# A hybrid decoder layer on one core: when the down projection's inputs are loaded, and where the output projection's inputs lie

## The chip, the core and the metric

The kernel runs on one core of one Trainium2 chip. The metric is the time of one execution on the device in microseconds. Before the change three runs took 2108.03, 2109.98 and 2113.12 us, so the median is 2109.98 us.

The core has five engines with a queue of instructions each, worked off in program order: PE multiplies matrices, DVE does elementwise arithmetic, ACT copies, casts and applies functions, POOL does elementwise work and issues DMAs, SP issues DMAs. An instruction that waits holds up everything behind it on its own engine. In the profile's tables PEld is PE's loading of weights, and POOLq or SPq is the part of an engine that issues DMAs.

## The reference

A decoder layer of 512 tokens (and 16 meta tokens) of width 2048: one input projection, eight heads of stick-breaking attention beside a gated short convolution of 1024 channels, one output projection, and a feed-forward part (SwiGLU) of width 5632, all in float32.

```python
n = _rmsnorm(h, g_mix[l])
p = n @ w_in[l]
...
o = jnp.concatenate([_rmsnorm(o_attn, g_attn_out[l]),
                     _rmsnorm(o_conv, g_conv_out[l])], axis=-1)
h = h + o @ w_out[l]

n2 = _rmsnorm(h, g_ffn[l])
h = h + (jax.nn.silu(n2 @ w_gate[l]) * (n2 @ w_up[l])) @ w_down[l]
```

## The kernel before

**Three passes for one product.** Every float32 operand is split into a high part (a cast on ACT) and the low rest (a subtraction on DVE). A product is three matmuls: high x high, high x low, low x high (lines 670 to 672 and 684 to 686). Activations lie in memory transposed, tokens along the free dimension, with their high and low parts side by side.

**Output projection.** `wide_product` (line 664) works on 512 tokens at a time. The attention heads' outputs are `oa`, the convolution's `oc`, each one block of 8 x 2 x 512 numbers per partition, made by `o_slots` (line 288). Where in a partition such a block begins is set by small pad tiles ahead of it and by an offset inside the tile: `oa` begins 16 bytes into its tile, `oc` at the start of its own. The weights' split tiles `s` do not move. The two results are scaled and added to the residual, which gives `h`; from `h` come the inputs of the feed-forward part, split into seven combinations `acts[0]` to `acts[6]`.

**Seven products in place of eight.** The feed-forward products use a scheme in which a 2x2 block product needs seven block products. For every output pair (two output tiles) four quads of weights are loaded by SP: b11, b12, b21, b22 (`load_quad`, line 577), one buffer for each. DVE forms from them t1 = b11 + b12, then t2 from t1 and b22, t3 = b12 + b22, and adds b21 to t2 (`prepare_pair`, line 619; sums on lines 606 and 613). Each of the seven resulting weights is split on ACT (line 599) and DVE (line 600) into one of three buffers `s`, about two blocks ahead of PE. A quad's buffer is loaded for the next pair as soon as its last reader is done.

**A pair on PE.** `pair_product` (line 688) runs seven blocks into three accumulators: x with acts 0, z with 1, x with 2, z with 3, x with 4, y with 5, x with 6. Between them ACT copies partial results out and DVE combines them (lines 709, 713, 716); the sum on line 716 is `c1`, and it follows block y. For gate and up a block is 8 tiles of 128, 24 matmuls; there are 44 such pairs. The down projection runs in four chunks over the 5632 rows, `CHUNKS = (5, 6, 5, 6)` tiles a block, each chunk with eight pairs; a block is then 15 or 18 matmuls. Results of the first three chunks are added to `hd` in DRAM by accumulating DMAs from POOL (lines 956 and 957), those of the last go out.

**From gate/up to down.** After every pair `gate` (line 872) forms the product of silu and up and `store_acts` (line 862) splits it and stores it to DRAM tensors `fd[chunk][s]`, s being 0 to 6, by DMAs on POOL (two for an even tile, five for an odd one). The down projection reads them back into twelve ring places of SBUF by `load_acts(c, s)` (line 890), two DMAs on POOL each: part 0 holds the high, part 1 the low halves. A chunk uses seven places, the next chunk the following seven, in a circle.

- Place 0 lies free; chunk 0's slot 0 is loaded during gate/up (line 912).
- Places 1 to 5 lie over the gate/up inputs `f01` and `f25`. These are two tiles with two inputs each: acts 0 and 1, acts 2 and 5 (line 741). Their loads are written after the gate/up loop (lines 916 to 918), ahead of the last `gate`.
- Place 6 lies over acts 3 and 4, the others over acts 6 and the gate's work tiles.
- The next chunk's slots 0 to 4 are asked for in pairs 1 to 5 of a chunk (line 933), slots 5 and 6 after the last pair (line 942).

**Who orders.** The program is written as a stream; a scheduler at build time fixes each engine's order by readiness in its own model and by priority, and places the semaphores. A DMA written later can therefore stand earlier in POOL's queue than the text suggests. A tile that takes over memory waits for the last reader of the tiles that lay there.

Of the kernel before, what the change touches and what calls it, by code (L numbers as in the profile page):

```python
# [32 lines left out]
def hybrid_layer(ctx: ExitStack, tc: tile.TileContext, xT, w_in, w_out, w_gu, w_down, vecs, out):  # L33
# [247 lines left out]
    kns = [apool.tile([P, 640], F32, name=f"kn{i}") for i in range(1)]  # L281
    for t in kns:
        gp.memset(t[:, L:640], 0.0)
    oapool.tile([P, 8], F32, name="pad_oa")
    acc_c = oapool.tile([P, SEQ], F32, name="acc_c")
    acc_a = oapool.tile([P, SEQ], F32, name="acc_a")

    def o_slots(pool, name, at):

        t = pool.tile([P, 2 * HEADS * SEQ + 8], F32R, name=name)[:, at : at + 2 * HEADS * SEQ]  # L290
        return t.rearrange("p (h a t) -> p h a t", h=HEADS, a=2)

    oa_all = o_slots(oapool, "oa", 4)
    oa = []

    def halves(ps, n):
# [210 lines left out]
    for j in range(HEADS):  # L507
        pc = pp.tile([P, 2, 512], F32, tag="pp", name=f"pc{j}")
        product([(pc[:, 0, :CH], C0, C0 + CH), (pc[:, 1, :CH], C0 + CH, L)], n_hl)
        cu = t512(2 * CH, "e", 2)[:, : 2 * CH]  # L510
        ve.tensor_tensor(two(cu), halves(pc, CH), two(r2[:, C0:]), ALU.mult)
        pu = pp.tile([P, 2, 512], F32, tag="pp", name=f"pu{j}")
        product([(pu[:, 0, :CH], C0, C0 + CH), (pu[:, 1, :CH], C0 + CH, L)], n_hl)
        ve.tensor_tensor(two(cu), halves(pu, CH), two(cu), ALU.mult)
        y = t512(SEQ, "e2", 2)[:, :SEQ]
        sc.activation(y, cu[:, 2 : 2 + SEQ], AF.Copy, scale=cw[:, 3 * j : 3 * j + 1])
        for t in (1, 2):
            ve.scalar_tensor_tensor(
                y, cu[:, 2 + t : 2 + t + SEQ], cw[:, 3 * j + t : 3 * j + t + 1], y, ALU.mult, ALU.add
            )  # L520
        pb = pp.tile([P, 2, 512], F32, tag="pp", name=f"pb{j}")
        product([(pb[:, 0, :], META, L)], n_hl)
        gb = t512(SEQ, "v", 2)[:, :SEQ]
        ve.tensor_tensor(gb, pb[:, 0, :], r[:, META:], ALU.mult)
        gp.tensor_tensor(y, y, gb, ALU.mult)
        g = g_cnv[:, j : j + 1]
        if j == 0:
            assert not waiting
            after(10, scale_a)
            apool.release()  # L530
            ocpool = open_pool("ocpool")
            ocpool.tile([P, 32], F32, name="pad_oc")
            oc_all = o_slots(ocpool, "oc", 0)
        oh, ol = oc_all[:, j, 0], oc_all[:, j, 1]
        sc.activation(oh, y, AF.Copy, scale=g)
        ve.scalar_tensor_tensor(ol, y, g, oh.bitcast(F32), ALU.mult, ALU.subtract)
        square_sum(acc_c, y, j == 0)
        oc.append((oh, ol))
# [195 lines left out]
    def slot(pool, dt, n, tag, name):  # L734
        return slots(pool, dt, 1, n, name, tag=tag)[0]
# [2 lines left out]
        pool.tile([P, n // 4], F32, name=f"pad_{pool.name}")  # L738

    acts = {}  # L740
    for a, b in ((0, 1), (2, 5)):
        acts[a], acts[b] = slots(fpool, F32R, 2, 8, f"f{a}{b}")
    pad(fpool, 160)
    fx = {i: dram.tile([P, 2, 8, T2], F32R, name=f"fx{i}") for i in (3, 4, 6)}
    for _ in range(4):
# [2 lines left out]
    def wide_tmp(tag, dt=F32, bufs=1):  # L748
        n_tmp[0] += 1
        return hbuf.tile([P, SEQ], dt, tag=tag, bufs=bufs, name=f"w{n_tmp[0]}")  # L750

    def scale_c():
        w = (wide_tmp("t1", F32R), wide_tmp("t2", F32R), wide_tmp("h", bufs=2), wide_tmp("r"), wide_tmp("s"))
        token_scale(acc_c, acc_c, 1024, "c", w)

    after(3, scale_c)
# [1 line left out]
    for i, j in enumerate(OUT_TILES):  # L758
        hj = wide_tmp("h", bufs=2)
        gp.dma_start(hj, xT[j][:, META:])  # L760
        if i + 1 < KT:
            ps_out.append(pp.tile([P, 2, 512], F32, tag="pp", name=f"po{i + 1}"))
            wide_product(ps_out[i + 1][:, 0, :], oa)
            wide_product(ps_out[i + 1][:, 1, :], oc)
        ps = ps_out[i]
        t1, t2 = wide_tmp("t1"), wide_tmp("t2")
        half, k = divmod(j, 8)
        if half == 1:

            src = hbuf.tile([P, 8, T2], F32, tag="src", name=f"src{k}")  # L770

        def residual(eng):
            ve.tensor_tensor(t1, ps[:, 0, :], acc_a, ALU.mult)
            eng.tensor_tensor(hj, hj, t1, ALU.add)
            ve.tensor_tensor(t2, ps[:, 1, :], acc_c, ALU.mult)
            eng.tensor_tensor(hj, hj, t2, ALU.add)
            sc.activation(src[:, 2 * half : 2 * half + 2], two(hj), AF.Copy, scale=g_ffn[:, j : j + 1])

        def split_f(s, i):
            split(acts[s][:, 0, k], acts[s][:, 1, k], src[:, i])  # L780

        def mixed_blocks():
            split_f(0, 0)
            ve.tensor_tensor(src[:, 4], src[:, 3], src[:, 1], ALU.subtract)
            split_f(1, 4)
            ve.scalar_tensor_tensor(src[:, 5], src[:, 4], -1.0, src[:, 0], ALU.mult, ALU.subtract)
            split_f(2, 5)
            ve.scalar_tensor_tensor(src[:, 6], src[:, 5], -1.0, src[:, 2], ALU.mult, ALU.subtract)
            ve.tensor_tensor(src[:, 7], src[:, 0], src[:, 1], ALU.subtract)

        if i == KT - 1:
            with tc.high_priority(1 << 20):
                residual(ve)
                square_sum(acc_h, hj, False, wide_tmp("s"))
                mixed_blocks()
            ocpool.release()
            oapool.release()
            fp = open_pool("fp")
            rings_p = [open_pool("ring_0")]
            pad(rings_p[0], 32)  # L800
            rings, n_ring, ring = {}, [0], []

            groups = {0: (0, 1), 1: (1, 2), 3: (1, 1), 4: (1, 1), 5: (1, 1), 6: (2, 1), 7: (2, 5)}

            def ring_place():
                i = n_ring[0] % 12
                n_ring[0] += 1
                if i == len(ring):
                    p, m = groups[i]
                    ring.extend(slots(rings_p[p], F32R, m, 6, f"ring{i}", tag=f"ring{i}"))  # L810
                return ring[i]

            r0 = ring_place()
            fpool_last = open_pool("fpool_last")
            for s, n in ((3, 7), (4, 7), (6, 8)):
                acts[s] = slot(fpool_last, F32R, 8, f"f{s}", f"f{s}")
                for part in range(2):
                    gp.dma_start(acts[s][:, part, :n], fx[s][:, part, :n], max_dma_last_dim=4096)
            split_f(3, 6)
            split_f(4, 7)  # L820
        else:
            residual(gp if half else ve)
            if half:
                split_f(5, 2)
                st = hbuf.tile([P, 2, 2, T2], F32R, tag="st", name=f"st{j}")[:, :, 0]
                split(st[:, 0], st[:, 1], src[:, 3])
                gp.dma_start(fx[6][:, :, k], st)
            else:
                mixed_blocks()
                st = hbuf.tile([P, 2, 2, T2], F32R, tag="st", name=f"st{j}")  # L830
                split(st[:, 0], st[:, 1], src[:, 6:8])
                for n, s in enumerate((3, 4)):
                    gp.dma_start(fx[s][:, :, k], st[:, :, n])
        if i < KT - 1:
            square_sum(acc_h, hj, i == 0, wide_tmp("s"))
        hd = dram.tile([P, SEQ], F32, name=f"hd{j}")
        (gp if i < KT - 1 else nc.sync).dma_start(hd, hj)
        hs[j] = hd
# [23 lines left out]
    def store_acts(blks, n, slots, kp):  # L862

        t = apool.tile([P, 2, n, T2], F32R, tag=f"s{n}", name=f"s{kp}_{n}")
        split(t[:, 0], t[:, 1], blks)
        c, k = at[kp]
        for i, s in enumerate(slots):
            gp.dma_start(fd[c][s][:, :, k], t[:, :, i])  # L868

    even = [None]  # L870

# [15 lines left out]
            ve.scalar_tensor_tensor(odd[:, 4], odd[:, 3], -1.0, odd[:, 0], ALU.mult, ALU.subtract)  # L887
            store_acts(odd, 5, (5, 6, 1, 2, 3), f // 2)

    def load_acts(c, s):  # L890
        if c < len(CHUNKS):
            n = CHUNKS[c]
            rings[c, s] = (ring_place() if c or s else r0)[:, :, :n]

            for part in range(2):
                gp.dma_start(rings[c, s][:, part], fd[c][s][:, part], max_dma_last_dim=3072)
# [17 lines left out]


    rings_p.append(open_pool("ring_a", side="right"))
    for s in range(1, 6):
        load_acts(0, s)
    pad(rings_p[1], 160)
    gate(FT - 1, g1, u1, x)  # L920
    apool.release()
# [4 lines left out]
    for c in range(len(CHUNKS)):  # L926
# [3 lines left out]
            hh = slots(rings_p[1], F32, 1, 6, "hh", tag="ring4")[0]  # L930
        for j in range(KT // 2):

            if 1 <= j <= 5:
                load_acts(c + 1, j - 1)
            c1 = cpool.tile([P, 2, T2], F32, tag="c1", name=f"d1_{c}_{j}")
            c2 = cpool.tile([P, 2, T2], F32, tag="c2", name=f"d2_{c}_{j}")
            if end:
                h2 = [hh[:, :, 2 * (j % 3) + m] for m in range(2)]
                for m in (1, 0):
                    gp.dma_start(h2[m], two(hs[2 * j + m]))  # L940
            x = pair_product([rings[c, s] for s in range(7)], c1, c2)
            if j == KT // 2 - 1:
                for s in (5, 6):
                    load_acts(c + 1, s)
# [74 lines left out]
```

## Time and profile before

| what | us |
|---|---|
| median of three runs | 2109.98 |
| the profiled execution | 2107.92 |
| its span, first to last instruction | 2106.2 |
| output projection on PE (from the first `wide_product` matmul) | 638.4 to 804.3 |
| gate and up | 804.3 to 1656.8 |
| down, chunk 0 | 1656.8 to 1768.7 |
| down, chunk 1 | 1768.7 to 1884.4 |
| down, chunk 2 | 1884.4 to 1985.6 |
| down, chunk 3 | 1985.6 to 2102.1 |

Lines of the views are read so: line of the kernel, engine, operation, output<-inputs by the program's names without numbers (so `s`, `ring`, `b` stand for all tiles of that name), shapes, count; then busy time and mean duration of one in ns. In timelines the first two numbers are start and duration, and the bracket holds the engine's idle time before it and what ended that. Matmuls overlap one another, so the mean duration of one (275 ns) is longer than the distance from one to the next.

### The profile page before, as it was taken

The page shows a single profiled execution, that of the slowest core. Times are in us where ns is not written, and L with a number is a line of the kernel's source. Part 1 is how long each engine was busy: PE and PEld are TensorE (multiplying, and loading weights), DVE is VectorE, ACT ScalarE, POOL GpSimd, SP SyncE. Part 2 cuts the span into 40 slices and gives each one's busy share as a digit, 9 for nine tenths or more (in the row PEclk, how much of TensorE's full clock was granted, in tenths as well). Part 3 has the DMA queues.
Part 4 walks back from the last instruction along what each step waited for, and adds up shares of the span by engine and source line. Part 5 has one row for each costly group of instructions (what it writes and reads, how often), then busy time and mean ns, then how long its engine had stood idle before and what let it go on. Part 6 is the DMA issues. An engine that isn't in the chain of part 4 may idle for free.

```text
span 2106.2 us, 39382 instructions
## 1 busy us (share of the span) xinstructions
PE 2070.5 (98%) x16086; PEld 1987.5 (94%) x16086; DVE 1644.0 (78%) x2131; ACT 1019.5 (48%) x1576; POOL 458.9 (22%) x584
## 2 busy tenths in 40 slices
PE   8999999999999999999999999999999899999999
PEld 7999999999998888999999999999999899999999
DVE  8777767433337669999999998999989777877798
ACT  6666666322224344555555554555555444444443
POOL 4111111010003544122121221221111323122232
PEclk9999999999999999999999999999999999999999
DMA  5222222222235556566565565565554999788863
GB/s 173 81 72 80 74 78 81 81 97 94 91 110 172 177 181 221 166 184 179 172 190 166 154 193 165 172 178 160 170 153 146 304 280 278 202 232 246 241 190 121
DMA packets 146006, 342.48 MB, mean 163 GB/s; under 512 B 13393, under 2 KB 58961, under 8 KB 145825
## 3 DMA queue, kind: packets, MB, share of 16 engines
q1 hardware_dynamic: 67824, 214.33, 32.1%
q0 software_dynamic: 78000, 125.63, 21.9%
q8 instruction: 126, 2.06, 0.4%
q14 instruction: 56, 0.45, 0.1%
HBM read 268.60 MB, written 71.30 MB: 161 GB/s over the span
## 4 chain that ended last, share of the span: by engine, by line
PE 87%; DVE 5%; DMA 4%; issue 2%; ACT 1%; POOL 0%; SPq 0%; DVEq 0%; ACTq 0%
PE x L684 10%; PE x L686 9%; PE x L685 9%; PE z L684 5%; PE z L685 5%; PE z L686 5%; PE y L686 3%; PE y L685 3%; PE y L684 3%; PE po L671 3%; PE po L670 3%; PE po L672 3%; DMA b<-w_down 2%; DVE s L600 2%; PE pv L168 2%
## 5 line engine op out<-in xcount | busy, mean ns | idle before, releaser
L599 ACT CAST s<-t 128x1024 fp32r<-128x1024 f32 (+2 forms) x304 | 286.3, 942 | 395.3 <-PE z L686 127.6
L600 DVE TENSOR_TENSOR s<-t,s 128x1024 fp32r<-128x1024 f32 (+2 forms) x304 | 343.4, 1129 | 94.0 <-ACT s L599 92.5
L686 PE MATMUL x<-f,s 128*128 128x256 f32 x1408 | 387.3, 275 | 1.5 <-DVE s L600 1.5
L685 PE MATMUL x<-f,s 128*128 128x256 f32 x1408 | 387.4, 275 | 1.3 <-DVE f L183 1.3
L684 PE MATMUL x<-f,s 128*128 128x256 f32 x1408 | 387.3, 275 | 0.2 <-ACT f L182 0.2
L599 ACT CAST s<-b 128x1024 fp32r<-128x1024 f32 (+2 forms) x228 | 214.7, 942 | 221.7 <-PE x L686 202.1
L686 PEld LDWEIGHTS x<-f,s 128*128 128x128 f32 x1408 | 264.3, 188 | 1.7 <-DVE s L600 1.7
L685 PEld LDWEIGHTS x<-f,s 128*128 128x128 f32 x1408 | 264.3, 188 | 1.7 <-DVE f L183 1.5
L684 PEld LDWEIGHTS x<-f,s 128*128 128x128 f32 x1408 | 264.3, 188 | 0.5 <-ACT f L182 0.4
L600 DVE TENSOR_TENSOR s<-b,s 128x1024 fp32r<-128x1024 f32 (+2 forms) x228 | 248.1, 1088 | 3.1 <-ACT s L599 2.5
L137 DVE TENSOR_TENSOR wlo<-raw,whi 128x512 fp32r<-128x512 f32 (+1 forms) x198 | 142.3, 720 | 130.9 <-ACT whi L136 130.3
L868 POOL DMA_DIRECT2D fd<-s x154 | 108.8, 921 | 583.6 <-DVE s L183 582.1
L136 ACT CAST whi<-raw 128x512 fp32r<-128x512 f32 (+1 forms) x198 | 121.3, 614 | 185.3 <-PE pu L170 65.5
L684 PE MATMUL x<-ring,s 128*128 128x256 f32 x704 | 195.7, 278 | 8.6 <-DVE d L713 5.6
L684 PE MATMUL z<-f,s 128*128 128x256 f32 x704 | 195.8, 278 | 3.3 <-ACT p L705 3.1
L685 PE MATMUL x<-ring,s 128*128 128x256 f32 x704 | 194.8, 277 | 3.3 <-DMA ring<-fd 3.3
L686 PE MATMUL x<-ring,s 128*128 128x256 f32 x704 | 195.0, 277 | 0.4 <-DVE s L600 0.4
L686 PE MATMUL z<-f,s 128*128 128x256 f32 x704 | 193.9, 275 | 0.0
L685 PE MATMUL z<-f,s 128*128 128x256 f32 x704 | 193.9, 275 | 0.0
L606 DVE TENSOR_TENSOR t<-b,b 128x1024 f32<-128x1024 f32 (+2 forms) x152 | 166.4, 1094 | 27.8 <-DMA b<-w_down 23.2
L684 PEld LDWEIGHTS x<-ring,s 128*128 128x128 f32 x704 | 132.7, 189 | 10.7 <-issue 8.5
L684 PEld LDWEIGHTS z<-f,s 128*128 128x128 f32 x704 | 132.1, 188 | 6.5 <-ACT p L705 6.3
(326 smaller groups left out, 5599.0 us busy)
## 6 DMA issues: line engine op xcount, KB each, us to landing
b<-w_gu SPq DMA_DIRECT2D x176, 512.0 KB, 3.6
raw<-w_in SPq DMA_DIRECT2D x92, 512.0 KB, 3.3
fd<-s POOLq DMA_DIRECT2D x154, 256.0 KB, 5.3
b<-w_down SPq DMA_DIRECT2D x64, 384.0 KB, 3.9
ring<-fd POOLq DMA_DIRECT2D x28, 768.0 KB, 12.2
b<-w_down SPq DMA_DIRECT2D x64, 320.0 KB, 4.8
ring<-fd POOLq DMA_DIRECT2D x28, 640.0 KB, 11.3
wide<-w_out SPq DMA_DIRECT2D x30, 512.0 KB, 3.4
```

Of the source, the lines that this page charges most:

```text
L136: sc.copy(hi[:, :c], raw)
L137: ve.tensor_tensor(lo[:, :c], raw, hi[:, :c].bitcast(F32), ALU.subtract)
L599: sc.copy(hi, src)
L600: ve.tensor_tensor(lo, src, hi.bitcast(F32), ALU.subtract)
L606: ve.tensor_tensor(sums[name], a, b, ALU.add)
L670: pe.matmul(ps, hi[:, kk], ah, start=k == 0, stop=False)
L671: pe.matmul(ps, hi[:, kk], al, start=False, stop=False)
L672: pe.matmul(ps, lo[:, kk], ah, start=False, stop=k == 7)
L684: pe.matmul(ps, hi[:, kk], act[:, 0, k], start=start and k == 0, stop=False, skip_group_check=not start)
L685: pe.matmul(ps, hi[:, kk], act[:, 1, k], start=False, stop=False, skip_group_check=not start)
L686: pe.matmul(ps, lo[:, kk], act[:, 0, k], start=False, stop=k == n - 1, skip_group_check=not start)
L868: gp.dma_start(fd[c][s][:, :, k], t[:, :, i])
```

## The change

Four things, as one diff:

- `oa` and `oc` lose the offset inside their tiles, and the pad ahead of `oa` grows.
- The inputs acts 0, 1, 2 and 5 get a tile each; acts 3 and 4 now share one. A temporary of `scale_c` moves into the tile `st`, which makes room for this.
- The loads of chunk 0's slots 1 to 5 get the highest priority, and the stores of the last gate/up pair's two tiles go out on SP in place of POOL.
- The next chunk's slots 0 to 4 are asked for in pairs 2 to 6, and each first has two elements written by ACT, copied from the `c1` of the pair before, so that its DMAs wait for that sum.

```diff
-    oapool.tile([P, 8], F32, name="pad_oa")
+    oapool.tile([P, 48], F32, name="pad_oa")
...
-    def o_slots(pool, name, at):
+    def o_slots(pool, name):
-        t = pool.tile([P, 2 * HEADS * SEQ + 8], F32R, name=name)[:, at : at + 2 * HEADS * SEQ]
+        t = pool.tile([P, 2 * HEADS * SEQ], F32R, name=name)
         return t.rearrange("p (h a t) -> p h a t", h=HEADS, a=2)
-    oa_all = o_slots(oapool, "oa", 4)
+    oa_all = o_slots(oapool, "oa")
...
-            ocpool.tile([P, 32], F32, name="pad_oc")
-            oc_all = o_slots(ocpool, "oc", 0)
+            oc_all = o_slots(ocpool, "oc")
...
-    for a, b in ((0, 1), (2, 5)):
-        acts[a], acts[b] = slots(fpool, F32R, 2, 8, f"f{a}{b}")
+    for i in (0, 1, 2, 5):
+        acts[i] = slot(fpool, F32R, 8, f"f{i}", f"f{i}")
...
+        v = hbuf.tile([P, 2 * SEQ], F32, tag="st", name="scale_v")
-        w = (wide_tmp("t1", F32R), wide_tmp("t2", F32R), wide_tmp("h", bufs=2), wide_tmp("r"), wide_tmp("s"))
+        w = (wide_tmp("t1", F32R), wide_tmp("t2", F32R), wide_tmp("h", bufs=2), v[:, :SEQ], wide_tmp("s"))
...
             fpool_last = open_pool("fpool_last")
+            acts[3], acts[4] = slots(fpool_last, F32R, 2, 8, "f34")
+            acts[6] = slot(fpool_last, F32R, 8, "f6", "f6")
             for s, n in ((3, 7), (4, 7), (6, 8)):
-                acts[s] = slot(fpool_last, F32R, 8, f"f{s}", f"f{s}")
...
         for i, s in enumerate(slots):
-            gp.dma_start(fd[c][s][:, :, k], t[:, :, i])
+            if kp < FT // 2 - 1:
+                gp.dma_start(fd[c][s][:, :, k], t[:, :, i])
+            else:
+                nc.sync.dma_start(fd[c][s][:, :, k].bitcast(F32), t[:, :, i].bitcast(F32))
...
-    def load_acts(c, s):
+    def load_acts(c, s, behind=None):
         if c < len(CHUNKS):
             n = CHUNKS[c]
             rings[c, s] = (ring_place() if c or s else r0)[:, :, :n]
+            if behind is not None:
+                sc.copy(rings[c, s][:1, :, 0, 0], behind[:1, :2])
...
-    for s in range(1, 6):
-        load_acts(0, s)
+    with tc.high_priority(1 << 20):
+        for s in range(1, 6):
+            load_acts(0, s)
...
-            if 1 <= j <= 5:
-                load_acts(c + 1, j - 1)
+            if 2 <= j <= 6:
+                load_acts(c + 1, j - 2, c1_last)
...
             x = pair_product([rings[c, s] for s in range(7)], c1, c2)
+            c1_last = c1[:, 0]
```

## The prediction

> **What bounds the kernel now.** I read first the page: the matrix engine (PE) is busy for nearly the whole span, and the chain of waits that ended last runs through it.
>
> ```profile
> span 2106.2 us, 39382 instructions
> PE 2070.5 (98%) x16086; PEld 1987.5 (94%) x16086; DVE 1644.0 (78%) x2131; ACT 1019.5 (48%) x1576; POOL 458.9 (22%) x584
> PE 87%; DVE 5%; DMA 4%; issue 2%; ACT 1%; POOL 0%; SPq 0%; DVEq 0%; ACTq 0%
> ```
>
> So only PE's holes can be won, and the rate of its matmuls. Next I cut the down projection into windows: the first three chunks, then single pairs of chunk 0 (six of its eight), then four pairs of chunk 2. The 76 output pairs are numbered through: 0 to 43 are gate/up, 44 to 51 chunk 0, 52 to 59 chunk 1, 60 to 67 chunk 2. Columns: start and end, length, busy time of PE, PEld, DVE, ACT, POOL with counts, granted clock, DMA share, GB/s. Pair borders are where the first matmul of a pair starts.
>
> ```profile
> 1656.80:1768.70 111.90, 100.99 (x842) 98.31 (x841) 82.00 (x117) 51.35 (x90) 32.03 (x41) 0.98 0.99 286
> 1768.70:1884.40 115.70, 114.90 (x1010) 114.54 (x1009) 91.65 (x114) 55.34 (x88) 25.14 (x32) 1.00 0.85 231
> 1884.40:1985.60 101.20, 97.19 (x842) 96.05 (x842) 78.77 (x112) 49.69 (x88) 23.20 (x30) 1.00 0.87 246
> ...
> 1656.80:1672.90 16.10, 11.54 (x78) 10.55 (x76) 11.06 (x16) 7.22 (x12) 6.35 (x10) 0.89 1.26 393
> 1672.90:1690.90 18.00, 16.58 (x134) 15.79 (x135) 11.25 (x16) 6.81 (x12) 7.10 (x9) 1.00 1.14 341
> 1690.90:1704.90 14.00, 12.55 (x108) 12.19 (x107) 10.09 (x17) 6.18 (x11) 4.74 (x6) 1.00 1.11 326
> 1704.90:1718.20 13.30, 12.40 (x107) 12.03 (x106) 9.53 (x15) 6.18 (x11) 3.27 (x4) 1.00 1.12 358
> 1730.10:1742.00 11.90, 11.90 (x107) 11.90 (x107) 10.02 (x15) 6.19 (x11) 1.70 (x2) 1.00 0.67 155
> 1753.90:1768.70 14.80, 12.22 (x107) 12.05 (x107) 10.34 (x15) 6.40 (x11) 5.43 (x7) 1.00 1.04 306
> ...
> 1884.40:1897.60 13.20, 12.55 (x107) 12.19 (x107) 9.35 (x15) 6.18 (x11) 5.15 (x7) 1.00 1.14 364
> 1897.60:1912.00 14.40, 12.48 (x107) 12.11 (x106) 9.67 (x15) 6.17 (x11) 4.02 (x6) 1.00 1.13 365
> 1912.00:1925.00 13.00, 12.43 (x108) 12.18 (x107) 9.73 (x15) 6.18 (x11) 1.72 (x2) 1.00 0.89 248
> 1972.60:1985.60 13.00, 12.14 (x107) 11.97 (x106) 10.20 (x15) 6.40 (x11) 5.44 (x8) 1.00 1.04 324
> ```
>
> A quiet pair of five tiles takes 11.9 us with PE full (7 blocks of 15 matmuls, 113 ns each, 1.7 us a block). Eight would be 95.2, so chunk 0 loses 16.7 us and chunk 2 loses 6.0. Chunk 1, whose matmuls need 1008 x 113 ns = 114.3 us, loses 1.4. Every losing pair has DMA at 300 GB/s or more (or, at 1912.0, its tail); the quiet pair has 155. Two things are late there. In the first pair it is the activations themselves (PE, timeline):
>
> ```profile
> 1660.35 0.35 PE L684 MATMUL x<-ring,s 128*128 128x256 f32 x1
> 1662.81 0.58 PE L685 MATMUL x<-ring,s 128*128 128x256 f32 x1 [2.10 <-DMA ring<-fd]
> 1666.89 0.39 PE L685 MATMUL z<-ring,s 128*128 128x256 f32 x1 [0.58 <-DMA ring<-fd]
> 1670.22 0.38 PE L685 MATMUL x<-ring,s 128*128 128x256 f32 x1 [1.23 <-DMA ring<-fd]
> ```
>
> In the other pairs it is the weights: a quad from w_down lands 6.5 us after issue while ring loads flow, 3.5 us in quiet pairs, and DVE, which adds quads in program order, stands still. The DMA views are of 1640 to 1690 and of 1725 to 1755; then DVE's longest such wait.
>
> ```profile
> ring<-fd POOLq DMA_DIRECT2D x12, 640.0 KB, 11.3
> b<-w_down SPq DMA_DIRECT2D x11, 320.0 KB, 6.5
> ...
> b<-w_down SPq DMA_DIRECT2D x9, 320.0 KB, 3.5
> ...
> 1699.09 0.82 DVE L606 TENSOR_TENSOR t<-b,b 128x640 f32<-128x640 f32 x1 [2.93 <-DMA b<-w_down]
> ```
>
> That wait of 2.93 us stands in the pair that loses 2.1, so about 0.9 us of such a wait is absorbed by the weights split ahead.
>
> **Part 1, the first loads (slots 1 to 6 of chunk 0).** POOL's timeline of before:
>
> ```profile
> 1646.60 1.40 POOL L868 DMA_DIRECT2D fd<-s  x2 [12.85 <-DVE s L183]
> 1647.78 3.09 POOL L896 DMA_DIRECT2D ring<-fd  x4
> 1654.53 1.42 POOL L896 DMA_DIRECT2D ring<-fd  x2 [3.66 <-PE y L686]
> 1656.74 2.85 POOL L896 DMA_DIRECT2D ring<-fd  x4 [0.79 <-issue]
> 1665.97 3.54 POOL L868 DMA_DIRECT2D fd<-s  x5 [6.38 <-DVE s L183]
> 1672.88 0.94 POOL L956 DMA_DIRECT2D hd<-d  x1 [3.37 <-DVE d L713]
> 1673.46 1.83 POOL L896 DMA_DIRECT2D ring<-fd  x2
> ```
>
> Slots 1 and 2 stand behind two stores, slot 3 behind the end of block y (tile f25 is shared by acts 2 and 5), slot 6 behind five stores that wait for DVE's split and one accumulation. After: tiles of their own, stores on SP, and in the built program's POOL order the twelve DMAs stand together ahead of the first accumulation. Their waits follow the blocks of the last gate/up pair, 24 matmuls or 2.7 us each: y, the sixth, ends by 1654.5, so f1 is free at 1643.5 and f2 at 1646.2. Slots 1 and 2 gain 4 us, slot 3 gains 8, slots 4 and 5 stay bound to f5 (1654.5), slot 6 goes from 1673.5 to about 1658. In the quoted PE rows the last parts of slots 2, 3 and 4 arrive at 1662.8, 1666.9 and 1670.2: four parts in 7.4 us, 1.85 us each. The first part should land 4 to 8 us after its issue (a weight quad of half the size takes 3.5 to 6.5), so at that cadence the twelfth lands 20.4 us after a first landing at 1648 to 1652: 1668 to 1672. That stands against uses that without waits begin at 1658.5 (slot 1) and then every 1.7 us up to about 1668 (slot 6, which the built order puts behind 25 matmuls of the next pair and of y). What is left of waiting for ring is 0 to 3 us, and 5 if the cadence is a quarter slower. The two pairs now take 34.1 us, 10.3 over quiet. DVE's busy 11.06 + 11.25 = 22.3 us in them (the last gate's work is in it) leaves 1.5 us of 23.8, so they won't be quiet: weights are still contended and the casts hand over with gaps. I take 29.0 for both, **5.1 us won**; bounds 1 (weights and DVE hold them) and 8.
>
> The seven stores (1.40 + 3.54 us of POOL) cost POOL nothing any more. On SP the first two stand behind a weight load and ahead of b21 of pair 44, three ahead of b21 of pair 45, two ahead of b11 of pair 46. By the built order each waits for a DVE split that stands earlier on DVE than the read that frees the next quad's buffer, so SP loses only issue time; but 256 KB each now travel in the weights' queue. That may bring back up to 2 us, inside the bounds above.
>
> **Part 2, one load a pair.** It removes the bursts after pair 45 and in pairs 60 to 62. Pairs 46 and 47 lose 2.1 + 1.4, pairs 60 to 62 lose 1.3 + 2.5 + 1.1, and of chunk 1's 1.4 I count 0.4, for its first pairs: **8.8 us**. The bursts in pairs 51 (2.9) and 67 (1.1) stay, since slots 5 and 6 are still loaded together there.
>
> What it adds: ten pairs of five tiles (46 to 50, 62 to 66) and five of six tiles each get two parts. In the built order the first goes out after the c1 sum of the pair before, the second behind that pair's last accumulation, so both lie in the stretch where the next pair's b12 and b22 are loaded. No row of before shows this alone. Bounds: 0 (two parts of 1.85 us fit into a DMA share of 0.67 per 11.9 us) and pair 61's 2.5. I take **0.5 each**, nearer to nothing because the DMA is not full, but not nothing because DVE has 1.9 us free in such a pair: 10 x 0.5 = 5.0. For the six-tile pairs 0.15, as now: 0.8. Net of part 2: 8.8 - 5.8 = **3.0 us won**.
>
> The hold itself is 15 ACT copies of two elements. The nearest row is a 128x256 copy:
>
> ```profile
> 1742.92 0.36 ACT L955 COPY d<-x 128x256 f32<-128x256 f32 x1
> ```
>
> ACT is busy 6.19 of 11.9 us, and the c1 sum that a copy waits for is done by the time the cast ahead of it in the built order (the next t1) ends; so the cast of t2 behind it is held up by 0.36 us at most. Cost 0; 15 x 0.36 = 5.4 us if every copy fell on the path. On POOL only accumulations stand behind a held load.
>
> **Part 3, the output projection.** Rows: mean ns of a 512-column matmul.
>
> ```profile
> L671 PE MATMUL po<-oa,s 128*128 128x512 f32 x120 | 47.6, 397 | 0.0
> L670 PE MATMUL po<-oc,s 128*128 128x512 f32 x120 | 47.1, 392 | 0.0
> L670 PE MATMUL po<-oa,s 128*128 128x512 f32 x120 | 47.0, 392 | 0.0
> L672 PE MATMUL po<-oc,s 128*128 128x512 f32 x120 | 47.0, 391 | 0.0
> L671 PE MATMUL po<-oc,s 128*128 128x512 f32 x120 | 46.7, 389 | 0.0
> L672 PE MATMUL po<-oa,s 128*128 128x512 f32 x120 | 46.6, 388 | 0.0
> ```
>
> oa takes 397 + 392 + 388 = 1177 ns for its three, oc 1172. oc does not move (byte 54400 of a partition); oa goes from 21488 to 21632, now a whole number of 64 bytes and exactly 32 KB below oc. Placed alike it should run alike: 5 ns x 120 = **0.6 us won**. Bounds from the extreme rows: all at 388 wins 1.6, all at 397 loses 1.7. The gate/up tiles move as well, but keep their 16-byte offset, and the same matmul out of tiles at quite other places has nearly one price:
>
> ```profile
> L685 PE MATMUL x<-f,s 128*128 128x256 f32 x1408 | 387.4, 275 | 1.3 <-DVE f L183 1.3
> L685 PE MATMUL x<-ring,s 128*128 128x256 f32 x704 | 194.8, 277 | 3.3 <-DMA ring<-fd 3.3
> ```
>
> So that move costs 0. The combined tile f34 waits for oc's last matmul, where f3 alone waited for oa's; its first use is four blocks on, so it costs nothing. scale_v is read before anything that reuses st.
>
> **Sum.** 5.1 + 3.0 + 0.6 = 8.7 us off the profiled execution's 2107.92 (span 2106.2 and 1.7 around it): 2099.2. The median of the runs shown is 2.1 above that execution, so 2099.2 to 2101.3; I say **2100**. Less than 0.2% (4.2 us) from 2109.98 can't be told from no change.
>
> **Rivals.**
> (a) The spread loads vanish in idle DMA, and the start wins 8: 8 + 8.8 + 0.6 = 17.4, 2090.5. For it: share 0.67. Against it: DVE's small reserve.
> (b) The start is held by weights, not by ring: it wins 1, the rest stays, 4.6 in all: 2103 to 2105. For it: DVE's 22.3 of 23.8; against it: the three ring waits alone are 3.9 us.
> (c) Slower: any ring part in flight delays b12 and b22 as much as a burst does, at each of the ten five-tile boundaries. At pair 46's 2.1 this is 21 + 0.8 - 8.8 - 5.1 - 0.6 = 7.3 more: 2115 to 2117. It decides from 1.4 us a boundary (no gain) and is measurably slower from 1.8. For it: pair 47, with three parts, loses 1.4; against it: in bursts the queue held more than two parts.
> The Trainium skill's page "DMA: Bandwidth & Descriptors", section "Queues, rings and completion order", has each DMA engine turn from queue to queue packet by packet, so a weight load would share with the ring queue however deep that is. The landing of 6.5 against 3.5 agrees that sharing costs; that depth is irrelevant no run here shows yet. By that rule (c).
> (d) The loads don't come earlier, since a wait not seen holds them: 3.0 + 0.6, 2104 to 2106.
>
> **Chances.** Forecast (its own range 2095 to 2104) 0.48; (a) 0.18; (b) 0.11; (c) 0.16; (d) 0.07. Faster: the forecast and (a) whole, 0.09 of (b), 0.03 of (d), together 0.78. Slower: 0.12 of (c). No change: what is left, 0.10. The range 2089 to 2110 holds the forecast, (b), (d), some 0.6 of (a) and the mild end of (c), about 0.8.
>
> **What will show it.** POOL's ring issues beginning near 1643.5 with no store ahead; PE's ring waits in the first pair below 2 us in sum and no clock of 0.89; pairs 44 and 45 near 29 us; pairs 46 to 50 near 12.4 with b12 landing 4 to 6 us after issue; L671 on oa at 389. Pairs 46 to 50 at 13.3 or more would make it wrong.

## The result and the profile after

The changed kernel takes 2120.79 us in the median, the kernel before, run beside it, 2112.44 us: a ratio of 1.0041, 95% interval 1.003 to 1.0052. It is 8.4 us slower where 2100 was forecast. The profiled execution of the changed kernel took 2119.01 us; of its page:

```profile
PE 2069.0 (98%) x16086; PEld 1985.2 (94%) x16086; DVE 1642.5 (78%) x2131; ACT 1022.1 (48%) x1591; POOL 456.7 (22%) x577
PE 81%; DVE 8%; DMA 7%; issue 3%; ACT 2%; SPq 0%; DVEq 0%; POOL 0%; ACTq 0%
```

The busy times are those of before. What grew is the share of DVE and DMA in the chain of waits, from 9% to 15% of the span. The windows say where (same columns as in the prediction; here several pairs stand in one row):

```profile
1657.00:1687.50 30.50, 26.61 (x213) 24.91 (x213) 22.54 (x34) 14.09 (x25) 5.87 (x8) 1.00 1.01 315
1687.50:1757.80 70.30, 62.13 (x528) 60.59 (x527) 48.55 (x71) 31.70 (x59) 15.76 (x20) 1.00 0.87 244
...
1888.70:1912.50 23.80, 23.80 (x212) 23.80 (x211) 19.34 (x28) 12.48 (x23) 3.80 (x5) 1.00 0.68 156
1912.50:1982.90 70.40, 62.53 (x528) 60.71 (x527) 48.84 (x72) 31.68 (x59) 15.78 (x20) 1.00 0.89 243
```

The rows are pairs 44 and 45, 46 to 50, 60 and 61, and 62 to 66. Beside the lengths of the same pairs before:

| pairs | what is loaded meanwhile, after | before | after |
|---|---|---|---|
| 44, 45 | chunk 0's own slots | 34.1 | 30.5 |
| 46 to 50 | one held load a pair | 63.0 | 70.3 |
| 51 | slots 5 and 6 | 14.8 | 14.9 |
| 52 to 59 (six tiles) | one held load in five of them | 115.7 | 116.0 |
| 60, 61 | nothing (before: a burst) | 27.6 | 23.8 |
| 62 to 66 | one held load a pair | 60.6 | 70.4 |
| 67 | slots 5 and 6 | 13.0 | 13.9 |

The start of the down projection won 3.6 us, and the bursts in pairs 60 and 61 are gone, another 3.8. But every pair of five tiles that carries one held load takes 13.5 to 14.8 us in place of the quiet 11.9. The ten of them cost 7.3 + 9.8 = 17.1 us more than before. Over these pairs the DMA share is 0.87 to 0.89; while one of the loads is in flight it is 1.05 (1715 to 1724), just behind that 0.75 (1724 to 1728). What DVE waits for in pairs 46 to 50 (its sums on line 605, and one of these waits in the timeline):

```profile
L605 DVE TENSOR_TENSOR t<-b,b x11: 824/826/827, 1687.4 to 1757.7; 128x640 f32<-128x640 f32 x11
...
  DMA b<-w_down: 15.3, 8
...
1723.66 0.82 DVE L605 TENSOR_TENSOR t<-b,b 128x640 f32<-128x640 f32 x1 [3.09 <-DMA b<-w_down]
```

Eight waits for a weight quad, 15.3 us in all; PE loses 70.3 - 59.5 = 10.8 us, for part of each wait is absorbed by the weights split ahead.

The two profiled executions differ by 11.1 us, the medians by 8.4. Part of that is chance: the first two gate/up pairs took 45.3 us in the profiled execution of before and 49.0 in hold_only below, whose code is the same up to there. PE waits for `fx` loads in these two pairs in every profiled execution but that of before (0.2 to 3.6 us, in hold_only 1.8), so before's was a lucky one there.

### The profile page after: what moved, and what is told of

Its sections match the earlier page's. It is cut to its first block, busy times and chain, and to the rows that moved or that the text cites. A ratio compares the mean times of both kernels' runs of the same rounds, so it can differ in the third digit from the quotient of the medians.

```text
span 2117.3 us, 39408 instructions
## 1 busy us (share of the span) xinstructions
PE 2069.0 (98%) x16086; PEld 1985.2 (94%) x16086; DVE 1642.5 (78%) x2131; ACT 1022.1 (48%) x1591; POOL 456.7 (22%) x577
## 4 chain that ended last, share of the span: by engine, by line
PE 81%; DVE 8%; DMA 7%; issue 3%; ACT 2%; SPq 0%; DVEq 0%; POOL 0%; ACTq 0%
PE x L683 8%; PE x L685 8%; PE x L684 8%; DMA b<-w_down 5%; PE z L683 4%; PE z L685 4%; PE z L684 4%; DVE s L599 3%; PE po L671 3%; PE po L670 3%; PE po L669 3%; PE y L685 2%; PE y L684 2%; PE y L683 2%; PE pv L168 2%
## 5 line engine op out<-in xcount | busy, mean ns | idle before, releaser
L870 POOL DMA_DIRECT2D fd<-s x147 | 103.8, 924 | 566.7 <-DVE s L183 565.2
L683 PEld LDWEIGHTS x<-ring,s 128*128 128x128 f32 x704 | 132.1, 188 | 19.3 <-ACT s L598 11.1
```

Of the source, the lines that this page charges most:

```text
L683: pe.matmul(ps, hi[:, kk], act[:, 0, k], start=start and k == 0, stop=False, skip_group_check=not start)
```

## The experiments

Theory H: a held load is in flight when the pair's weight quads b12 and b22 are, delays them, and costs some 2 us a pair, whatever its size. Rival R1: the loss comes from the other edits. Further rivals were the ScalarE copy that holds the loads, the bytes, and full DMA engines. Ratios are against the kernel before, run on the same chip, with 95% intervals. Not all kernels ran on one chip, so two of them are compared by their ratios.

| kernel | median us | ratio | pairs 44, 45 | 46 to 50 | 60, 61 | 62 to 66 |
|---|---|---|---|---|---|---|
| before | | 1 | 34.1 | 63.0 | 27.6 | 60.6 |
| the change | 2120.79 | 1.0041 (1.003 to 1.0052) | 30.5 | 70.3 | 23.8 | 70.4 |
| no_hold | 2109.32 | 0.9987 (0.9977 to 0.9998) | 31.1 | 63.1 | 28.0 | 60.4 |
| hold_only | 2127.76 | 1.0079 (1.0063 to 1.0095) | 33.0 | 70.5 | 23.8 | 69.5 |
| first_only | 2110.49 | 0.9999 (0.999 to 1.0008) | 30.5 | 64.5 | 27.0 | 61.2 |
| first_again | 2109.77 | 1.0 (0.9991 to 1.001) | 31.7 | 63.1 | 27.0 | 61.5 |
| oproj_only | 2109.27 | 0.9992 (0.9981 to 1.0002) | 34.0 | 62.9 | 27.7 | 60.8 |
| held_small | 2110.06 | 0.9999 (0.9988 to 1.001) | 30.6 | 68.2 | 24.2 | 59.5 |
| two_a_pair | 2113.85 | 1.0011 (1.0001 to 1.002) | 32.5 | 65.1 | 23.8 | 67.3 |
| late | 2123.82 | 1.0061 (1.0045 to 1.0077) | 31.6 | 71.2 | 23.8 | 70.8 |
| pool_b22 | 2100.97 | 0.9957 (0.9939 to 0.9975) | 30.9 | 59.5 | 23.8 | 61.0 |
| sp_b22 | 2097.20 | 0.9933 (0.9919 to 0.9946) | 30.0 | 59.5 | 23.8 | 59.5 |
| all_b22 | 2098.60 | 0.9946 (0.9933 to 0.9958) | 30.2 | 60.7 | 27.5 | 59.9 |

### Which edit it is: no_hold and hold_only

The hold is the copy on ACT and the shift by one pair. no_hold is the changed kernel without it, by the edit shown; hold_only is the kernel before with the opposite edit alone:

```diff
-            if 2 <= j <= 6:
-                load_acts(c + 1, j - 2, c1_last)
+            if 1 <= j <= 5:
+                load_acts(c + 1, j - 1)
```

> The changed kernel with its hold undone: the next chunk's loads are issued as before, in bursts from the second pair of a chunk, without the ScalarE copy. Theory H (each load held to one pair delays that pair's weight quads, and the price is per pair touched, about 2.1 us a boundary): pairs 46 to 50 fall from 70.3 us to about 63, pairs 62 to 66 from 70.4 to about 61, pairs 60 and 61 rise from 23.8 to about 27.6, and the time comes 14 us down, to about 2106, some 0.3% below the kernel before. Rival R1 (the loss comes from the moved tiles, the stores on SyncE or the two-block tile f34, not from the hold): the time stays above 2116 and pairs 46 to 50 above 68 us. Rival R2 (bursts cost the same bytes and so the same time, only elsewhere): the pairs change places but the sum of pairs 44 to 67 stays within 3 us of the changed kernel's 339.8.

> The kernel before with nothing but the hold: one load a pair from the third pair of a chunk, each behind the ScalarE copy of the pair before. Theory H: pairs 46 to 50 go from 63.0 us to about 70, pairs 62 to 66 from 60.6 to about 70, pairs 60 and 61 from 27.6 to 23.8, the time to about 2126, 0.6 to 0.7% above the kernel before. Rival R1 (the hold is harmless by itself and the loss comes from the other edits or from their meeting with it): within 0.2% of the kernel before.

The windows of pairs 46 to 50, 60 and 61, and 62 to 66 of no_hold:

```profile
1688.90:1752.00 63.10, 61.00 (x527) 60.10 (x527) 48.86 (x71) 30.91 (x55) 12.35 (x15) 1.00 0.88 252
...
1883.50:1911.50 28.00, 25.08 (x213) 24.35 (x212) 19.09 (x29) 12.35 (x22) 9.11 (x12) 1.00 1.13 361
1911.50:1971.90 60.40, 59.80 (x527) 59.63 (x526) 49.46 (x70) 30.95 (x55) 8.62 (x10) 1.00 0.69 170
```

and of pairs 46 to 50 and 62 to 66 of hold_only, with the first two gate/up pairs ahead of them:

```profile
804.30:853.30 49.00, 42.70 (x340) 41.04 (x339) 41.01 (x47) 23.48 (x34) 17.53 (x15) 0.97 0.71 236
...
1692.90:1763.40 70.50, 62.94 (x528) 61.90 (x527) 49.49 (x73) 31.78 (x60) 16.15 (x20) 0.98 0.88 246
...
1919.50:1989.00 69.50, 61.70 (x527) 60.37 (x527) 48.74 (x72) 31.69 (x59) 15.67 (x20) 1.00 0.87 246
```

The hold goes with the long pairs in both directions. By itself it costs 16.7 us in the medians (2127.76 against 2111.07), inside the change 11.5 (2120.79 against 2109.32; by the two ratios 11.4). Why the two differ is not shown; in hold_only's profile the clock is lower in places (0.97 in the row of the first gate/up pairs). R1 falls, and so does R2: without the hold pairs 44 to 67 take 327.3 us in all against 339.8. The change without its hold is 0.1% faster than before; 14 us had been expected of taking it back, 11.5 came.

### What in the hold it is: held_small and two_a_pair

held_small was to keep the copy, its wait and the issues, and to move a sixth of the bytes in one chunk:

```diff
-                gp.dma_start(rings[c, s][:, part], fd[c][s][:, part], max_dma_last_dim=3072)
+                k = n - 1 if behind is not None and c == 3 else 0
+                gp.dma_start(rings[c, s][:, part, k:], fd[c][s][:, part, k:], max_dma_last_dim=3072)
```

> The changed kernel, where the loads that are held in the third chunk (pairs 62 to 66) move one block of six; the chunk that reads them computes with old blocks. The ScalarE copy, its wait and the issues on GpSimd stay. Theory H (the loads' bytes in flight delay b12 and b22): pairs 62 to 66 fall from 70.4 us to 60 to 61, pairs 46 to 50, whose loads are whole, stay at 70. Rival W (the copy that waits on ScalarE, or the issues in GpSimd's order, makes the loss): pairs 62 to 66 stay at 69 to 71.

The edit does more than that. The copy writes into the first block of a ring place, and the load now fills the last block alone, so it no longer waits for the copy. All ten small loads go out from 1877.4 to 1891.2, in pairs 59 and 60, and pairs 62 to 66, which begin at 1910.2, have no load in flight (POOL's first issue of them, then the DMA issues of 1872 to 1892):

```profile
1877.37 1.09 POOL L904 DMA_DIRECT2D ring<-fd  x2 [0.96 <-PE x L685]
...
ring<-fd POOLq DMA_DIRECT2D x10, 128.0 KB, 7.3
```

Pairs 62 to 66 of held_small, then the DMA issues of that stretch:

```profile
1910.20:1969.70 59.50, 59.50 (x527) 59.50 (x526) 50.26 (x71) 31.31 (x59) 8.59 (x10) 1.00 0.66 155
```

```profile
b<-w_down SPq DMA_DIRECT2D x19, 320.0 KB, 3.5
```

The same pairs of the changed kernel (DMA issues from 1912 to 1983):

```profile
ring<-fd POOLq DMA_DIRECT2D x10, 768.0 KB, 9.1
b<-w_down SPq DMA_DIRECT2D x19, 320.0 KB, 6.5
```

Pairs 46 to 50, whose loads are whole and held, stay long (68.2, a little under the 70 expected). Pairs 62 to 66 are quiet, PE without a hole, with the copies in them and no load. So the copies alone cost nothing. In the changed kernel ACT does stand at ten of the fifteen, 10.5 us in all; here for 1.36 us (ACT's timeline of the changed kernel):

```profile
1714.47 0.20 ACT L900 CAST ring<-d 1x2 fp32r<-1x2 f32 x1 [1.36 <-DVE d L715]
1715.60 0.73 ACT L598 CAST s<-t 128x640 fp32r<-128x640 f32 x1 [0.93 <-PE x L685]
```

The cast behind the copy waits for PE in any case. What goes with the long pairs is that quads land later: 6.5 us after their issue in place of 3.5 in pairs 62 to 66, a median over quads of which two in four are late. Since held_small has no load at all in these pairs, it tells neither bytes from presence nor the loads from their issues on POOL. two_a_pair bears on the first, pool_b22 on the second: it issues ten loads from POOL in ten pairs and loses 1.5 us in all.

two_a_pair has the same bytes in three pairs:

```diff
-            if 2 <= j <= 6:
-                load_acts(c + 1, j - 2, c1_last)
+            if 2 <= j <= 4:
+                for s in ((0, 1), (2, 3), (4,))[j - 2]:
+                    load_acts(c + 1, s, c1_last)
```

> The changed kernel with the same loads, held two to a pair, in three pairs instead of five. Theory H (the price is 2.1 us for each pair whose weight quads meet a load, whatever its bytes): pairs 46 to 50 and 62 to 66 come to 65 to 67 us each, the time to about 2112. Rival B (the price goes with the bytes that are moved beside weights): both stay at 69 to 71, the time at 2119 or more.

Its pairs 46 to 48, then 62 to 64, one by one:

```profile
1689.40:1703.30 13.90, 12.46 (x108) 12.10 (x107) 9.91 (x16) 6.47 (x13) 4.71 (x7) 1.00 1.06 321
1703.30:1716.80 13.50, 12.45 (x107) 12.09 (x106) 9.61 (x15) 6.37 (x12) 4.67 (x7) 1.00 1.12 359
1716.80:1730.70 13.90, 12.49 (x107) 12.13 (x107) 9.64 (x15) 6.18 (x11) 2.88 (x4) 1.00 0.97 293
...
1911.40:1926.10 14.70, 12.53 (x107) 12.17 (x106) 9.97 (x16) 6.46 (x13) 4.79 (x7) 1.00 1.06 318
1926.10:1941.20 15.10, 12.54 (x108) 12.17 (x107) 9.73 (x15) 6.38 (x12) 4.73 (x7) 1.00 1.12 343
1941.20:1954.90 13.70, 12.46 (x108) 12.09 (x107) 9.69 (x15) 6.18 (x11) 2.82 (x4) 1.00 0.90 260
```

A pair with four parts (the first two of each three) loses 2.0, 1.6, 2.8 and 3.2 us, one with two parts (the third) 2.0 and 1.8. In the mean that is 2.4 against 1.9 us for twice the bytes. The price goes nearly by the pair that meets a load and not by the byte, and rival B falls. So to spread the same bytes over more pairs is to pay more often, and a burst, which packs them into the fewest pairs, is cheaper. In pairs 62 to 66 the loss is 7.8 us, 0.3 beyond the range expected, and the time came 1.9 above the 2112.

### When a load costs nothing: late, sp_b22 and pool_b22

late holds a load behind c2's first half in place of c1:

```diff
-            if 2 <= j <= 6:
-                load_acts(c + 1, j - 2, c1_last)
...
             x = pair_product([rings[c, s] for s in range(7)], c1, c2)
+            if 1 <= j <= 5:
+                load_acts(c + 1, j - 1, c2[:, 0])
```

> The changed kernel with each load held to the middle of a pair, behind the first half of c2 (some 7 us into the pair), where b12 and b22 of the pair have landed, instead of its start. Theory H (what is lost is b12's and b22's slack): the load meets b11 and b21, which have longer, and its tail meets b12 of the next pair; pairs 46 to 50 and 62 to 66 come to 62 to 66 us each, the time to 2105 to 2112. Rival T (any load in flight in a pair costs the pair 2 us, since the DMA engines are full): both stay at 69 or more.

This missed: 71.2 us. Its POOL and DVE timelines say why:

```profile
1698.09 1.48 POOL L903 DMA_DIRECT2D ring<-fd  x2 [7.39 <-ACT ring L900]
```

```profile
1710.45 0.83 DVE L605 TENSOR_TENSOR t<-b,b 128x640 f32<-128x640 f32 x1 [3.75 <-DMA b<-w_down]
1725.70 0.83 DVE L605 TENSOR_TENSOR t<-b,b 128x640 f32<-128x640 f32 x1 [4.21 <-DMA b<-w_down]
```

The load goes out 9.8 us after the start of pair 46 (1688.3), not 7: the copy on ACT waits for the sum of c2, and that sum stands on DVE behind the pair's own late weights. So each load is in flight when the next pair's b12 is issued, and DVE waits 3.75 and 4.21 us for that. Thus late moved the load from one pair's b12 to the next one's; what a load in the middle of a pair does it could not show. The next kernel can.

sp_b22 issues each load on SP, in program order right behind b22 of the next pair, held by a copy from the split of b22:

```diff
                 split_quad(b["22"], n)
                 load_quad(i + 1, "22")
+                while later:
+                    load_acts(*later.pop(), split_w[-1][1], nc.sync)
...
             if 2 <= j <= 6:
-                load_acts(c + 1, j - 2, c1_last)
+                later.append((c + 1, j - 2))
```

> The changed kernel with each of the next chunk's loads issued on SyncE's queue right behind b22 of the next pair, one load a pair, instead of on GpSimd's queue; the copy that holds them now reads the split of b22. Theory H (a load costs because it shares the engines with b12 and b22 from another queue): on the same queue it is moved after them, only b21 and b11 come behind it, and pairs 46 to 50 and 62 to 66 come to 59.5 to 62 us each, pairs 60 and 61 stay at 23.8, the time comes to 2102 to 2106. Rival T (the engines are full): 66 us or more each, b11 or b21 being late in the place of b12.

SP's timeline in pair 47 of sp_b22 (the first row holds b12 and b22, the last b21 and the following b11), its DMA issues in pairs 46 to 50, and the windows of the ten pairs:

```profile
1700.92 2.87 SPq L581 DMA_DIRECT2D b<-w_down  x2
1703.84 0.94 SPq L910 DMA_DIRECT2D ring<-fd  x2
1707.20 3.67 SPq L581 DMA_DIRECT2D b<-w_down  x2
```

```profile
ring<-fd SPq DMA_DIRECT2D x10, 768.0 KB, 7.0
b<-w_down SPq DMA_DIRECT2D x20, 320.0 KB, 4.8
```

```profile
1688.00:1747.50 59.50, 59.50 (x527) 59.50 (x527) 49.45 (x70) 31.57 (x60) 8.56 (x10) 1.00 0.95 286
...
1901.30:1960.80 59.50, 59.50 (x527) 59.50 (x526) 49.74 (x71) 31.57 (x60) 8.58 (x10) 1.00 0.96 287
```

All ten pairs are quiet with a load in each, at more bytes a second (286 against 244 GB/s) and a higher DMA share (0.95 against 0.87) than the changed kernel had. So rival T falls: over a pair there was room for the load, and its place in the pair was wrong. This kernel takes 2097.20 us, 0.67% less than before (0.54 to 0.81) and the lowest median of all.

Is it the queue or the moment? pool_b22 issues at the same moment from POOL:

```diff
-                    load_acts(*later.pop(), split_w[-1][1], nc.sync)
+                    load_acts(*later.pop(), split_w[-1][1])
```

> The kernel of sp_b22 with the held loads issued from GpSimd's queue again, at the same time: behind the copy of b22's split. Theory M (the moment decides: a load may not be in flight while b12 is): pairs 46 to 50 and 62 to 66 stay at 59.5 to 61 us each, the time at 2097 to 2100. Theory Q (the queue decides: beside the weights' queue a load takes half of the engines, behind it none): b22, which is issued with the load, lands 6 us after its issue instead of 4 and comes late, pairs 46 to 50 and 62 to 66 go to 64 to 68 us each, the time to 2106 to 2114.

Its ten pairs:

```profile
1688.40:1747.90 59.50, 59.50 (x527) 59.50 (x527) 49.42 (x70) 31.56 (x60) 16.43 (x20) 1.00 1.03 285
...
1901.10:1962.10 61.00, 60.04 (x527) 59.68 (x526) 49.52 (x71) 31.41 (x60) 16.42 (x20) 1.00 1.00 279
```

The moment, almost alone: nine pairs are at 11.9 us and one, in which b21 landed 8.2 us after its issue, loses 1.5. Theory Q falls in this form. The ratio, 0.9957, is 0.0024 above sp_b22's, which was taken on another chip, and the two intervals overlap, so whether the queue adds something stays open.

What each quad pays stands in the traces, load by load. From issue to landing, medians in us over pairs 46 to 50 and 62 to 66 (of held_small only the latter five; SP issues the quads in the order b11, b12, b22, b21):

| kernel | b11 | b12 | b22 | b21 |
|---|---|---|---|---|
| held_small, no load | 3.5 | 3.7 | 3.5 | 2.8 |
| the change | 3.5 | 6.8 | 7.0 | 3.7 |
| late | 7.3 | 7.5 | 6.2 | 2.8 |
| sp_b22 | 5.7 | 4.3 | 4.2 | 6.0 |
| pool_b22 | 5.8 | 4.4 | 4.1 | 6.4 |

A load slows whatever quads are in flight beside it, in every placement. Where b12 is among them PE has holes in each pair; where it is b21 and b11 instead, PE is full in nineteen pairs of twenty. These two have the slack.

### The other edits: first_only, first_again and oproj_only

first_only is the kernel before with the input tiles parted, f34, the last stores on SP, the early loads of slots 1 to 5 and scale_v; first_again is the same kernel. oproj_only has the pads and offsets of the output projection and scale_v.

> The kernel before with the first loads alone: separate tiles for the feed-forward blocks, f34, the seven last stores on SyncE, the first ring loads ahead of the last gate (and the scratch row scale_v shared, without which it does not fit). Theory H: pairs 44 and 45 fall from 34.1 us to 30.5 as in the changed kernel, nothing else moves, ratio about 0.998 to 0.9985. Rival R3 (what the first loads win is given back in the first gate/up pair, which is 1.6 us longer in the changed kernel, because of f34): that pair is at 22 us here too, and the ratio is 0.999 to 1.0.

> The first loads alone once more, since its time and its profile do not agree (0.9999 of the kernel before, 3.5 us less in pairs 44 to 67): if the profile is right, 0.998 to 0.999 here and 325 to 327 us in pairs 44 to 67; if not, 1.0 and 328 or more.

> The kernel before with the output projection's tiles moved alone (and scale_v). Theory H: all six groups of the output projection at 226 to 227 ns from start to start, so the stage goes from 165.9 us to about 163.5, 2.4 us won, ratio about 0.999. Rival R3 (the first gate/up pair waits for its last loads of fx whatever the stage before won): that pair is 1 to 1.6 us longer, and 0.8 to 1.4 us of the 2.4 remain, which 5 rounds do not tell from nothing.

Pairs 44 and 45 win 3.6 us in first_only and 2.4 in first_again; of the 3.6, 1.5 are lost in the next five. Over pairs 44 to 67 the profiles are 3.4 and 1.3 below before (first_again's 327.5 lies between the two cases expected). The times show nothing (0.9999 and 1.0, each to 0.1%). So the early first loads are worth between nothing and some 2 us. R3 is not decided: the first gate/up pair is long, as it says (23.3 and 23.0 us against 20.7), but the second is shorter (23.1 and 23.3 against 24.6), and the two together, 46.4, lie between the 45.3 of before and the 49.0 of hold_only, whose code is that of before there. PE waits 2.7 and 2.5 us for `fx` loads in these pairs; but it waits 1.8 in hold_only and 0.9 in oproj_only as well, which have no f34, so that f34 is the reason is not shown.

The output projection from 645 to 795 us: the same 150 us hold 655 matmuls before and 663 after (PE rows of before, then of the change).

```profile
645.00:795.00 150.00, 150.00 (x655) 122.53 (x654) 105.47 (x143) 60.69 (x98) 69.24 (x75) 1.00 0.59 179
```

```profile
645.00:795.00 150.00, 150.00 (x663) 124.20 (x662) 107.35 (x145) 61.07 (x98) 70.60 (x77) 1.00 0.60 180
```

That is 229.0 against 226.2 ns, 2.8 x 720 = 2.0 us won; oproj_only has 663 too. By operand, from one start to the next in the order of the lines, the groups of before take 230.2, 236.3 and 225.7 ns on oa and 230.4, 227.1 and 228.8 on oc; in oproj_only all six take 226.4 to 227.0, as expected. Its first two gate/up pairs take 48.1 us, and its time (0.9992, 0.9981 to 1.0002) can't be told from no change. Of the 2.0 us about 1 is left in the mean where the down projection begins: at 1657.4 us in the ten profiles with this edit, at 1658.4 in the four without it (these from 1656.8, which is before, to 1659.9).

### The rest of the bursts: all_b22 and two_queues

Slots 5 and 6 are still loaded together in the last pair of a chunk. all_b22 puts slot 5 behind b22 of that pair's successor too, slot 6 one pair later:

```diff
-            if 2 <= j <= 6:
-                later.append((c + 1, j - 2))
+            if 2 <= j <= 6 or j == KT // 2 - 1:
+                later.append((c + 1, min(j - 2, 5)))
+            if j == 0 and c:
+                later.append((c, 6))
...
-            if j == KT // 2 - 1:
-                for s in (5, 6):
-                    load_acts(c + 1, s)
```

> The kernel of sp_b22, with blocks 5 and 6 of the next chunk moved to SyncE's queue too, behind b22 of the last pair and of the next chunk's first, where they were a burst of four parts from GpSimd in the last pair. If the burst's meeting with b12 and b22 is what lengthens pairs 51, 67 and 68 (15.1, 14.8 and 16.7 us against 11.9, 11.9 and 14.3): they come to 12 to 12.5, 12 to 12.5 and 14.3 to 15, some 6 us in all, and the time to about 2091. Rival: block 6 lands too late for the first pair of the third chunk, which waits 1 to 3 us there, and half or less of it remains, 2094 to 2097.

Pair 51, then pairs 60 and 61:

```profile
1748.80:1760.70 11.90, 11.90 (x107) 11.90 (x106) 10.25 (x15) 6.54 (x12) 1.72 (x2) 1.00 0.99 308
1875.00:1902.50 27.50, 25.96 (x213) 25.59 (x212) 19.77 (x28) 12.51 (x23) 3.44 (x4) 0.94 0.71 181
```

Pair 51 is quiet, pair 67 at 12.2, but pairs 60 and 61 take 3.7 us more than in sp_b22. That is the rival: PE waits 0.4 and 1.1 us for parts of the ring there, and the clock is 0.94. Pair 68 takes 17.6 us where 14.3 to 15 were expected, and no gain over sp_b22 shows in the time. two_queues was to load slot 6 from POOL at the moment of slot 5 (edit against all_b22):

```diff
-            if 2 <= j <= 6 or j == KT // 2 - 1:
-                later.append((c + 1, min(j - 2, 5)))
-            if j == 0 and c:
-                later.append((c, 6))
+            if 2 <= j <= 6:
+                later.append((c + 1, j - 2))
+            elif j == KT // 2 - 1:
+                later += [(c + 1, 5), (c + 1, 6)]
...
-                    load_acts(*later.pop(), split_w[-1][1], nc.sync)
+                    k = later.pop(0)
+                    load_acts(*k, split_w[-1][1], None if k[1] == 6 else nc.sync)
```

> The kernel of sp_b22, with the last pair's burst of blocks 5 and 6 split: block 5 behind b22 on SyncE's queue, block 6 from GpSimd's queue at the same moment (held by the same split). If what lengthens pairs 51, 67 and 68 and, in all_b22, pairs 60 and 61 is b12 meeting a load or block 6 coming too late: neither happens here; b22 shares with two parts only, as in pool_b22. Pairs 51 and 67 come to 12 to 13.5 us, pairs 60 and 61 stay at 23.8 to 25, and the time comes to 2092 to 2096. Rival: b22 late by 2 us in each of the three last pairs, pairs 51 and 67 stay at 14 or more and the time at 2097.

In it the load of slot 6 is written ahead of the second product of the last pair, whose place it takes; that product works on the new block and waits for it (PE's timeline):

```profile
1764.52 0.58 PE L687 MATMUL z<-ring,s 128*128 128x256 f32 x1 [6.07 <-DMA ring<-fd]
```

It takes 2132.35 us (ratio 1.0092, 1.0078 to 1.0107), which says nothing of the question. What the last pairs' bursts can yield (3 us in each of pairs 51 and 67 of sp_b22) stays open.

## Why the prediction was wrong, point by point

**The step that failed** is in part 2: "I take 0.5 each, nearer to nothing because the DMA is not full, but not nothing because DVE has 1.9 us free in such a pair". Each of the ten boundaries cost 2.2: pairs 46 to 50 and 62 to 66 take 140.7 us, 21.7 over quiet, in place of 5.0. That is 16.7 of the 19.8 us between the sum's 2099.2 and the profiled execution's 2119.0. b12 landed 5.8 to 8.2 us after its issue, in the median 6.8, where 4 to 6 were forecast. The first ground was beside the matter: a mean share of 0.67 says that the bytes fit (sp_b22 shows it, with PE full at 0.95), but not that a quad lands in time, and while the load is in flight the share is 1.05. The second is weak because DVE works in order: what stands behind the sum that waits for b12 can't fill the wait.

**What the step removes was right**: 8.8 us were counted for the bursts, 0.4 of them in chunk 1, and no_hold's pairs 46 to 50, 60 and 61, and 62 to 66 hold 3.6 + 4.2 + 0.9 = 8.7 over quiet. The hold copies at 0 were right (held_small's pairs 62 to 66), though the reason given was not: in the changed kernel the sum is often not done, and ACT waits.

**Rival (c) was what happened**, its place and its price of 2.1 a boundary included; its 2115 to 2117 lie 2 us below the profiled execution's 2119.0. Its chance was set too low by the argument that "in bursts the queue held more than two parts". In two_a_pair b12 landed 6.5 to 6.9 us after its issue beside four parts, 6.7 and 7.3 beside two, so between these depth made no difference to it. That agrees with the Trainium skill's page "DMA: Bandwidth & Descriptors", section "Queues, rings and completion order", by which each DMA engine takes turns between queues that have work. The warning limit set, 13.3 us for pairs 46 to 50, was passed at 14.1.

**Part 1** came in its signs and not in its size. POOL's timeline of the changed kernel:

```profile
1643.91 4.30 POOL L903 DMA_DIRECT2D ring<-fd  x6 [9.90 <-PE z L685]
1654.80 1.42 POOL L903 DMA_DIRECT2D ring<-fd  x2 [6.58 <-PE y L685]
1657.00 2.85 POOL L903 DMA_DIRECT2D ring<-fd  x4 [0.79 <-issue]
```

Slots 1 to 3 go out from 1643.9 (1643.5 forecast), slot 6 by 1659; PE waits once for ring, 1.13 us, and the clock is 1.00. The two pairs took 30.5 us, not 29.0: weights are late there still (DVE waits 3.3 us for quads). The 3.6 won lie inside the bounds of 1 to 8. What the stage won the time does not show.

**Part 3** was mis-sized: 2.0 us in the stage, not 0.6. oa won more than the 5 ns forecast for its three matmuls (in the change their distances sum to 680 ns, before to 692), and oc's became faster too (680 against 686), though oc does not move. The bounds, 1.6 won at most, were drawn for oa alone and from mean durations of single matmuls, which overlap; the distance from one to the next (229.0 to 226.2 ns, by counting) is what the stage pays.

With the three terms put right, 2107.92 - 3.6 - (8.8 - 21.7 - 0.8) - 2.0 = 2116.0; of the 3.0 left to 2119.0, 1.0 lies in the first two gate/up pairs (46.3 against 45.3), 0.9 in the rest of gate and up (852.5 us in all before, 854.4 after) and 1.0 in pairs 51 and 67. Two slips in the prediction's figures change nothing in it: 1008 x 113 ns is 113.9 us (114.3 goes with 113.4 ns), and 2.93 less 2.1 is 0.8, not 0.9.

## What to carry to other kernels

Spare DMA bandwidth does not make a transfer free: ask which load has the least slack between its issue and its use, and put bulk transfers behind it, not beside it. Where any overlap delays that load by about the same amount, however little else is queued, spreading the bulk thin is the worst schedule, a burst is better, and a place right after the critical issue is best: here ratios of 1.0041, 0.9987 and 0.9933. A mean share over a pair, of DVE or of the DMA engines, says nothing of a wait early in the pair.

## What was not expected of the hardware

- Two of oc's three matmul groups ran faster (230.4 and 228.8 ns before, 226.6 and 227.0 in oproj_only) though neither oc nor the split weights changed their addresses. Why is not settled.
- The mean granted clock was 0.79 in a pair of two_queues in which PE stood still for 6 us at once, as against 1.00 in the changed kernel's pairs of 14 us with their shorter holes (windows of two_queues below). The longest hole alone does not tell it: the first down pair of before had 0.89 with none above 2.10 us.

```profile
1747.90:1771.10 23.20, 13.69 (x89) 12.61 (x89) 7.74 (x11) 4.73 (x10) 3.20 (x4) 0.79 0.79 256
```

- The same code differs from one execution to the next by as much as the changes that were being measured: hold_only's first two gate/up pairs had a clock of 0.97 and took 3.7 us more than those of before.
